# The second feed-forward product in chunks of 2, 3, 2, 2 pairs in place of 2, 2, 2, 3, with fetches for the next chunk begun in a chunk's first unit

## The chip, the core and the metric

The kernel runs on one core of a Trainium2 chip. The metric is the device time of one launch in microseconds (us), as the median of several runs. The engines are named as in the profile: PE multiplies matrices, ACT and DVE work on elements, POOL starts the accumulating transfers, and SP starts nearly all other transfers.

## What is computed

The reference is a decoder trunk of two layers over a stream of 1024 tokens by 1024 features in float32. Each layer has a mixer (in layer 0 a gated convolution beside a matrix memory, in layer 1 a gated unit) and then the feed-forward part, which is all that the change touches:

```python
def swiglu(xn, w_in, w_out):          # xn 1024 x 1024, D_FF = 2816
    h = xn @ w_in
    g, up = h[..., :D_FF], h[..., D_FF:]
    return (jax.nn.silu(g) * up) @ w_out

for layer in range(2):
    x = x + mixer(rmsnorm(x, norm_mix[layer]), ...)
    x = x + swiglu(rmsnorm(x, norm_ffn[layer]), ffn_w_in[layer], ffn_w_out[layer])
return rmsnorm(x, norm_final)
```

## The kernel before

Every float32 product is made of three passes over operands that are cut into a high part (rounded to the fast float32 format) and a low part (the rest): high by high, high by low, low by high. They are the lines 121, 122 and 123, so a "matmul" below is one of these passes, of 128 x 128 weights on 512 columns.

The 2816 hidden features are 22 blocks of 128. The first product makes them block by block. Blocks 0 to 17 form nine pairs, and for these the second product is done by a scheme of seven block products in place of eight: `STEPS` names them, and each takes one of seven sums of weight blocks and one of seven sums of hidden blocks (b11, b21, t2, t1, t3, b22, t4; below, block 0 to 6). The seven sums of hidden blocks of a pair are stored, high and low, in DRAM (`hd`), 14 tiles of 256 KB per pair. Blocks 18 to 21 (the tail, `TAIL = 4`) go through DRAM too (`td`, 16 tiles in all), and are multiplied in the ordinary way at the end (`part`, tiles f0y, weights by line 109).

The second product runs over chunks of pairs, and `PAIRS` says how many pairs each chunk has. In a chunk there are four units (`onto(dp, ch)`, dp = 0 to 3), each of which makes two of the eight row blocks of the output. A unit runs the seven steps; a step has three matmuls for each pair, so that a unit has 42 matmuls in a chunk of two pairs and 63 in a chunk of three. Three PSUM banks a unit (A, B, C) take the products; the function `sink` copies (line 497), subtracts (line 500) or adds (line 490) them. The first chunk leaves its results in the 16 tiles f0x. In every later chunk two of a unit's four results are built in fresh tiles f0e, and POOL adds each to its f0x tile by an accumulating transfer (line 394, `gather`).

For each unit two raw weight tiles st0 and st1 are fetched by SP (line 323). ACT and DVE cut and sum them one unit ahead of their use (lines 329, 330 and 340 to 343). The raw tiles have four buffers, so that the tiles of one unit can be fetched only when DVE is through with those of the unit two before it.

The hidden blocks of a chunk are fetched by SP as well: `bring(ch, i)` fetches block i of chunk ch, two tiles for each of its pairs (line 479, tiles f0h), into a pool of 68 tiles called slots. That pool also holds the 16 f0x tiles and the f0e tiles. A chunk of two pairs needs 28 slots and one of three pairs 42. The tables `spread` and `ending` say after which step of which unit each block of the next chunk (with `ending`, of the tail) is called for. Each entry stands for a unit, and has steps and the blocks called for after them. A scheduler then fixes the order of the instructions on each engine at build time; each engine runs its own in that order and waits on semaphores, and SP too starts its transfers strictly in order.

Names: f0h is followed by pair, block and part (0 high, 1 low), as in f0h630 for pair 6, block 3, high; st0_f0o31 is the first raw weight tile of chunk 3, unit 1; f0e31 is the result tile of row block 3, right half. Layer 1 has the same with f1.

Of the kernel before, what the change touches and what calls it, by code (L numbers as in the profile page):

```python
# [23 lines left out]
NC = S // P  # L24
SLOT = 516
EPS = 1e-6
PAIRS = (2, 2, 2, 3)
TAIL = 4
DIRECT = 2
GELU_C = math.sqrt(2.0 / math.pi)  # L30
# [13 lines left out]
def trunk(ctx, tc, x_t, vecs, b_gate, b_s, ws_t, we, we_v, we_g, we_o, wo_u, wo_v, wo_o, wf_in, wf_out, out_t):  # L44
# [351 lines left out]
    def swiglu(layer, normed, todo, spans, after):  # L396
# [80 lines left out]
        def fetch(at, i, nm):  # L477
            t = slot(nm, F32R)
            nc.sync.dma_start(t[:, :HALF].bitcast(F32), at[i * P : (i + 1) * P, :])
            return t  # L480
# [3 lines left out]
        def onto(dp, ch):  # L484
# [14 lines left out]
            def less(d, c, p, q):  # L499
                nc.vector.tensor_tensor(hold[d, c], p, q, op=ALU.subtract)  # L500
                if not opening:
                    gather(x[d][c][:, :HALF], hold[d, c])

            def sink(s, ps):
# [9 lines left out]
                else:  # L514
                    less(d0, 1, ps, hold[d0, 1])
                if s == 6 and ch == len(PAIRS) - 1:
                    for d in rows:
# [7 lines left out]

        firsts = [sum(PAIRS[:ch]) for ch in range(len(PAIRS))]
        hbs = [{} for _ in PAIRS]
        hl = [[None, None] for _ in range(TAIL)]

        def bring(ch, i):  # L530

            if ch < len(PAIRS):
                hbs[ch][BLOCKS[i]] = [
                    tuple(fetch(hd[p], 2 * i + j, f"{name}h{p}{i}{j}") for j in range(2))
                    for p in range(firsts[ch], firsts[ch] + PAIRS[ch])
                ]
# [13 lines left out]
            w = Halves(wf_in[layer, f], wf_in[layer, NF + f], HALF, f"{name}i{f}")  # L550
            units.append((w, xb, into(f), none if f < NF - 1 else early(0, {s: (s,) for s in range(7)})))
        base = 0
        spread = ({}, {2: (0,), 5: (1,)}, {2: (2,)}, {0: (3,), 2: (4,), 4: (5,), 5: (6,)})
        ending = ({}, {}, {2: (0,)}, {1: (1,)})
        for ch, n in enumerate(PAIRS):
            for dp in range(4):
# [528 lines left out]
    n1, n2, n3 = Scaled("ffn0"), Norm("mix1", True, spill), Scaled("ffn1")  # L1085
    x, todo = even(n1)
    x, todo = swiglu(0, n1, todo, halves, n2)
    x, todo = odd(n2, todo, n3)
    x, todo = swiglu(1, n3, todo, thirds, Final())
    for step in todo:  # L1090
        step()
# [60 lines left out]
```

## Time and profile before

| | us |
|---|---|
| median of three runs | 2099.26 (2099.06 to 2102.05) |
| the profiled execution | 2099.18 |
| its span in the trace | 2097.5 |
| PE busy in the span | 2075.4 (99%) |
| DVE, ACT, POOL busy | 1376.9 (66%), 825.0 (39%), 277.2 (13%) |

The profile is one execution. Its span is from the first to the last instruction seen, and its own time lies 1.68 us above the span. A busy share is time in which the engine had an instruction running; a PE that is busy can still be slow, which the granted clock shows (a mean of 0.996 over the span).

### The profile page before, as it was taken

To read this page: it belongs to the slowest core of one execution; us is meant where nothing else is said; L and a number is where in the kernel's file an instruction comes from. 1 tells how busy PE (TensorE), PEld (TensorE's weight loads), DVE (VectorE), ACT (ScalarE), POOL (GpSimd) and SP (SyncE) were. 2 spreads that over 40 slices of the span, in tenths; PEclk is the share of its full clock that TensorE was granted. 3 is DMA by queue.
4 is the path that set the end of the run, shared out by engine and by line. 5 is a ranking of instruction groups with operands and counts; after the bars stand their busy time and mean duration, and the time that the engine had idled before them with its cause. 6 is when DMAs were issued, how large, how long until landed. Compare 5 with 4: busy or idle time off the path is not lost.

```text
span 2097.5 us, 25504 instructions
## 1 busy us (share of the span) xinstructions
PE 2075.4 (99%) x9294; PEld 1680.6 (80%) x9294; DVE 1376.9 (66%) x2176; ACT 825.0 (39%) x1277; POOL 277.2 (13%) x453
## 2 busy tenths in 40 slices
PE   9999999999999999999999999999999999999998
PEld 7878888888888878877778888888888888877777
DVE  6236566568877777666556666666877777656566
ACT  5111112345444444343235743445444444433234
POOL 0000000003222121101231000002212112001120
PEclk9999999999999999999999999999999999999999
DMA  5121111545444344479994221445534434379993
GB/s 172 61 76 61 46 51 51 189 142 122 179 152 160 131 158 157 156 279 277 309 253 158 91 71 41 169 158 116 184 128 161 160 126 169 114 273 306 322 231 97
DMA packets 131935, 327.89 MB, mean 156 GB/s; under 512 B 17073, under 2 KB 19153, under 8 KB 131809
## 3 DMA queue, kind: packets, MB, share of 16 engines
q1 hardware_dynamic: 88912, 209.77, 29.2%
q0 software_dynamic: 42752, 116.46, 19.2%
q8 instruction: 73, 1.20, 0.2%
q14 instruction: 54, 0.43, 0.1%
q10 hardware_dynamic: 144, 0.03, 0.0%
HBM read 213.98 MB, written 91.24 MB: 146 GB/s over the span
## 4 chain that ended last, share of the span: by engine, by line
PE 89%; issue 5%; DMA 4%; DVE 1%; POOL 1%; ACT 0%; SPq 0%; DVEq 0%; POOLq 0%; ACTq 0%
PE Af1i L121 4%; PE Af1i L122 4%; PE Af1i L123 4%; PE Af0i L121 2%; PE Af0i L122 2%; PE Af0i L123 2%; PE Bf1i L121 2%; PE Bf1i L123 2%; PE Bf1i L122 2%; PE Af1o L121 2%; PE Af1o L123 1%; PE Af1o L122 1%; PE ov L121 1%; PE op L121 1%; PE ou L121 1%
## 5 line engine op out<-in xcount | busy, mean ns | idle before, releaser
L260 POOL DMA_DIRECT2D x_dram<-xe x16 | 8.6, 540 | 450.8 <-DVE xe L274 445.7
L260 POOL DMA_DIRECT2D x_dram<-xo x16 | 8.6, 540 | 276.8 <-DVE xo L274 271.7
L110 ACT CAST hi_eo<-st_eo 128x1024 fp32r<-128x1024 f32 x20 | 21.0, 1049 | 48.9 <-PE ep L122 30.6
L459 DVE TENSOR_TENSOR f0q<-f0q,Af0i 128x512 f32<-128x512 f32 x20 | 13.8, 688 | 35.9 <-PE Af0i L123 35.9
L459 DVE TENSOR_TENSOR f1q<-f1q,Af1i 128x512 f32<-128x512 f32 x20 | 13.7, 687 | 35.7 <-PE Af1i L123 35.7
L394 POOL DMA_DIRECT2D f0x<-f0e x24 | 20.7, 874 | 120.3 <-DVE f0e L500 103.7
L394 POOL DMA_DIRECT2D f1x<-f1e x24 | 21.0, 878 | 117.9 <-DVE f1e L500 95.3
L329 ACT CAST hix_f0i<-st_f0i 128x1024 fp32r<-128x1024 f32 x20 | 21.1, 1053 | 39.2 <-PE Af0i L122 25.1
L329 ACT CAST hix_f1i<-st_f1i 128x1024 fp32r<-128x1024 f32 x20 | 21.0, 1052 | 38.5 <-PE Af1i L122 25.1
L329 ACT CAST hiy_f1i<-st_f1i 128x1024 fp32r<-128x1024 f32 x20 | 21.1, 1053 | 31.3 <-PE Bf1i L122 30.7
L329 ACT CAST hiy_f0i<-st_f0i 128x1024 fp32r<-128x1024 f32 x20 | 21.1, 1055 | 31.1 <-PE Bf0i L122 30.6
L449 DVE TENSOR_TENSOR f1b<-Cf1i,f1b 128x512 f32<-128x512 f32 x20 | 13.8, 689 | 26.6 <-issue 17.9
L449 DVE TENSOR_TENSOR f0b<-Cf0i,f0b 128x512 f32<-128x512 f32 x20 | 13.8, 688 | 26.6 <-issue 17.9
L121 PE MATMUL f1y<-f1h,hi_f1o 128*128 128x256 f32 (+1 forms) x96 | 30.8, 321 | 0.0
L122 PE MATMUL f1y<-f1h,hi_f1o 128*128 128x256 f32 (+1 forms) x96 | 30.8, 321 | 0.0
L110 ACT CAST hi_oo<-st_oo 128x1024 fp32r<-128x1024 f32 x16 | 16.8, 1052 | 35.1 <-PE op L122 26.9
L123 PE MATMUL f1y<-f1h,lo_f1o 128*128 128x256 f32 (+1 forms) x96 | 30.6, 319 | 0.0
L110 ACT CAST hi_evw<-st_evw 128x1024 fp32r<-128x1024 f32 x8 | 8.4, 1050 | 55.5 <-PE ek L122 36.6
L329 ACT CAST hia_f1i<-st_f1i 128x1024 fp32r<-128x1024 f32 x20 | 21.0, 1050 | 22.2 <-PE Cf1i L122 18.4
L329 ACT CAST hia_f0i<-st_f0i 128x1024 fp32r<-128x1024 f32 x20 | 21.0, 1049 | 22.2 <-PE Cf0i L122 18.4
L111 DVE TENSOR_TENSOR lo_eo<-st_eo,hi_eo 128x1024 fp32r<-128x1024 f32 x20 | 24.5, 1223 | 7.5 <-ACT hi_eo L110 7.5
L274 DVE TENSOR_TENSOR xe<-ep,xe 128x512 f32<-128x512 f32 x16 | 11.0, 690 | 27.5 <-PE ep L123 27.4
(3189 smaller groups left out, 7405.5 us busy)
## 6 DMA issues: line engine op xcount, KB each, us to landing
f0h<-hd SPq DMA_DIRECT2D x126, 256.0 KB, 5.8
f1h<-hd SPq DMA_DIRECT2D x126, 256.0 KB, 5.8
st_f0i<-wf_in SPq DMA_DIRECT2D x40, 512.0 KB, 3.5
st_f1i<-wf_in SPq DMA_DIRECT2D x40, 512.0 KB, 3.4
st_eo<-we_o SPq DMA_DIRECT2D x16, 512.0 KB, 3.7
st_oo<-wo_o SPq DMA_DIRECT2D x16, 512.0 KB, 3.5
st_f0o<-wf_out SPq DMA_DIRECT2D x24, 256.0 KB, 3.5
f0x<-f0e POOLq DMA_DIRECT2D x24, 256.0 KB, 6.6
```

Source lines behind the costliest of these rows:

```text
L110: nc.scalar.copy(hi[:, part], st[:, part])
L111: nc.vector.tensor_tensor(lo[:, part], st[:, part], hi[:, part].bitcast(F32), op=ALU.subtract)
L121: nc.tensor.matmul(ps, lhsT=lh, rhs=rh, start=first, stop=False, skip_group_check=more)
L122: nc.tensor.matmul(ps, lhsT=lh, rhs=rl, start=False, stop=False, skip_group_check=more)
L123: nc.tensor.matmul(ps, lhsT=ll, rhs=rh, start=False, stop=last, skip_group_check=more)
L260: nc.gpsimd.dma_start(x_at[0][d * P : (d + 1) * P, c * HALF : (c + 1) * HALF], x[d][c][:, :HALF])
L274: nc.vector.tensor_tensor(x, ps, x, op=ALU.add)
L329: nc.scalar.copy(hi, src)
L394: nc.gpsimd.dma_start(dst, src, accum_op=ALU.add)
L449: nc.vector.tensor_tensor(r, ps, r, op=ALU.add)
L459: nc.vector.tensor_tensor(st["q"], st["q"], ps, op=ALU.subtract)
```

## The change

The chunk of three pairs moves from the last place to the second, and the table of the fetches is a new one. The weights of the second product are laid out by the host from `PAIRS`, so they follow.

```diff
-PAIRS = (2, 2, 2, 3)
+PAIRS = (2, 3, 2, 2)
...
-        spread = ({}, {2: (0,), 5: (1,)}, {2: (2,)}, {0: (3,), 2: (4,), 4: (5,), 5: (6,)})
+        spread = ({5: (0,)}, {2: (1,), 5: (2,)}, {2: (3,)}, {2: (4,), 4: (5,), 5: (6,)})
         ending = ({}, {}, {2: (0,)}, {1: (1,)})
```

Before, block 0 of the next chunk was called for in the second unit, and blocks 3 to 6 in the last. Now block 0 is called for in the first unit, block 3 in the third, and blocks 4 to 6 in the last. The table for the tail stays. Both layers are built alike.

What this makes of the order on SP, at the fetches for the chunk of three pairs: before, that is chunk 3, whose blocks 3 to 6 (24 tiles) stand between the weights of its first and of its second unit.

```order
L323 DMA st0_f0o30_81_7989<-wf_out 128x768
L323 DMA st1_f0o30_81_7990<-wf_out 128x768
L479 DMA f0h630_8003<-hd06_3431 128x512
L479 DMA f0h631_8005<-hd06_3431 128x512
...
L479 DMA f0h860_8103<-hd08_3433 128x512
L479 DMA f0h861_8105<-hd08_3433 128x512
L323 DMA st0_f0o31_82_8118<-wf_out 128x768
L323 DMA st1_f0o31_82_8119<-wf_out 128x768
```

After, it is chunk 1; the same place in the program reads:

```order
L323 DMA st0_f0o10_73_7241<-wf_out 128x768
L323 DMA st1_f0o10_73_7242<-wf_out 128x768
L479 DMA f0h230_7182<-hd02_3427 128x512
...
L479 DMA f0h431_7192<-hd04_3429 128x512
L323 DMA st0_f0o11_74_7358<-wf_out 128x768
L323 DMA st1_f0o11_74_7359<-wf_out 128x768
L479 DMA f0h240_7275<-hd02_3427 128x512
L479 DMA f0h241_7277<-hd02_3427 128x512
...
L479 DMA f0h461_7344<-hd04_3429 128x512
L323 DMA st0_f0o12_75_7468<-wf_out 128x768
```

Six fetches (block 3) stand behind the weights of the first unit, then come the weights of the second unit, and 18 fetches (blocks 4 to 6) follow them.

On ACT, at the second unit of chunk 1, before (a chunk of two pairs); DMAHW names a transfer started by SP, DMASW one started by POOL, and the others the engines:

```order
L497 COPY f0e21_7442<-Af0o11_74_7415 128x512 [waits PE_49]
L329 CAST hix_f0o12_75_7473<-st0_f0o12_75_7411 128x512 [waits DVE_49,PE_49,Activation_49]
L497 COPY f0e31_7458<-Bf0o11_74_7416 128x512 [waits DMAHW6_49]
L329 CAST hiy_f0o12_75_7485<-st1_f0o12_75_7412 128x512 [waits DMAHW5_49,PE_49]
L329 CAST hiz_f0o12_75_7504<-s3_f0o12_75_7468 128x256 [waits PE_49]
```

And after (a chunk of three pairs):

```order
L497 COPY f0e21_7508<-Af0o11_74_7472 128x512 [waits PE_49]
L497 COPY f0e31_7527<-Bf0o11_74_7473 128x512 [waits DMASW1_49,DVE_49,PE_49]
L329 CAST hix_f0o12_75_7545<-st0_f0o12_75_7468 128x768 [waits DVE_49,PE_49,Activation_49]
L329 CAST hiy_f0o12_75_7560<-st1_f0o12_75_7469 128x768 [waits DMAHW7_49,PE_49]
L329 CAST hiz_f0o12_75_7582<-s3_f0o12_75_7540 128x384 [waits PE_49]
```

The copy that makes f0e31 stood behind the first cut of the next unit's weights and waited for an SP transfer; now it stands ahead of that cut and waits for a POOL transfer, which is the accumulating transfer of f0e01, made by the unit before, whose slot it takes.

## Rows read from the trace of the kernel before

**Rows 1.** Page, busy time of each engine: us, share of span, instructions.
```profile
PE 2075.4 (99%) x9294; PEld 1680.6 (80%) x9294; DVE 1376.9 (66%) x2176; ACT 825.0 (39%) x1277; POOL 277.2 (13%) x453
```

**Rows 2.** Windows, layer 0: stretch, busy us, granted PE clock, DMA share, GB/s.
```profile
917.00:927.00 10.00, 10.00 (x43) 7.67 (x43) 5.91 (x11) 4.40 (x9) 0.00 (x0) 1.00 0.69 227
...
1007.00:1017.00 10.00, 10.00 (x45) 8.09 (x44) 7.19 (x12) 3.15 (x5) 1.72 (x2) 1.00 1.07 346
...
1027.00:1037.00 10.00, 7.31 (x26) 4.42 (x25) 1.07 (x2) 0.90 (x2) 1.09 (x2) 0.95 1.07 329
1037.00:1047.00 10.00, 10.00 (x32) 7.68 (x32) 9.93 (x17) 3.41 (x5) 4.12 (x5) 0.71 0.84 149
```

**Rows 3.** Timeline of PE, layer 0: start, duration, instruction, idle time before it.
```profile
877.92 0.39 PE L121 MATMUL Af0i<-x_ffn000h,hia_f0i 128*128 128x512 f32 x1
...
897.34 0.39 PE L121 MATMUL Af0o<-f0h,hia_f0o 128*128 128x512 f32 x1
...
1030.43 0.40 PE L121 MATMUL Af0o<-f0h,hiy_f0o 128*128 128x512 f32 x1
...
1036.64 0.80 PE L121 MATMUL Af0o<-f0h,hia_f0o 128*128 128x512 f32 x1 [1.99 <-ACT hia_f0o L329]
...
1043.13 0.40 PE L121 MATMUL Cf0o<-f0h,hia_f0o 128*128 128x512 f32 x1
...
1051.92 0.39 PE L123 MATMUL Bf0o<-f0h,lox_f0o 128*128 128x512 f32 x1
1052.64 0.50 PE L121 MATMUL Af0o<-f0h,hiy_f0o 128*128 128x512 f32 x1 [0.34 <-DVE f0e L500]
```

**Rows 4.** Timeline of PE, layer 1, the same place.
```profile
1985.09 0.47 PE L121 MATMUL Af1o<-f1h,hiy_f1o 128*128 128x512 f32 x1
...
1991.92 0.79 PE L121 MATMUL Af1o<-f1h,hia_f1o 128*128 128x512 f32 x1 [2.34 <-ACT hia_f1o L329]
...
1995.44 0.39 PE L123 MATMUL Af1o<-f1h,loa_f1o 128*128 128x512 f32 x1
```

**Rows 5.** Chain of waits, 1000 to 1060 us: start, duration, what.
```profile
1020.12 5.56 DMA f0h<-hd
1025.74 9.99 DMA st_f0o<-wf_out
1035.75 0.84 ACT hia_f0o L329
...
1042.18 0.87 DVE lox_f0o L330
```

**Rows 6.** Timeline of SP's queue, layer 0: transfers started, grouped.
```profile
931.41 8.90 SPq L479 DMA_DIRECT2D f0h<-hd  x16
...
989.82 12.79 SPq L479 DMA_DIRECT2D f0h<-hd  x18
...
1004.34 20.72 SPq L479 DMA_DIRECT2D f0h<-hd  x24
1025.74 18.54 SPq L323 DMA_DIRECT2D st_f0o<-wf_out  x6
1053.48 1.97 SPq L109 DMA_DIRECT2D st_f0o<-wf_out  x2
1055.50 21.30 SPq L479 DMA_DIRECT2D f0h<-td  x16
```

**Rows 7.** Line 479 (fetches of hidden blocks), 900 to 1090 us: issue to landing.
```profile
DMA to landing us min/median/max: 2.9/5.9/11.7
```

**Rows 8.** Timeline of PE in layer 0, chunk 1.
```profile
954.44 0.40 PE L121 MATMUL Af0o<-f0h,hiz_f0o 128*128 128x512 f32 x1
```

**Rows 9.** Timeline of POOL: the second accumulating transfer of chunk 1.
```profile
949.36 0.86 POOL L394 DMA_DIRECT2D f0x<-f0e  x1 [0.46 <-DVE f0e L500]
```

**Rows 10.** Tile f0e, 940 to 1000 us: its 11 accumulating transfers, issue to landing.
```profile
DMA to landing us min/median/max: 4.0/5.3/7.8
```

**Rows 11.** Tile f0e, 900 to 1090 us: all 24 of layer 0.
```profile
DMA to landing us min/median/max: 3.6/6.6/13.3
```

## Prediction

> **What bounds the kernel now.** I began with the busy times of the page. PE runs in 2075.4 of 2097.5 us [rows 1], so an edit that moves no work off PE can only win time in which PE waits, or in which it runs at the lower clock. The second step was to find such time in the stretch that the change touches, the second product. On PE's timeline the pitch of undisturbed matmuls comes from the last unit of the first product: 84 matmuls lie between 877.92 and 897.34, which is 0.2312 us each [rows 3]. Against this pitch there is one large loss in layer 0. From 1030.43 to 1043.13 PE starts 24 matmuls in 12.70 us [rows 3]; at the pitch they take 24 x 0.2312 = 5.55, so **7.15 us** are lost. Part of it is idle time, 1.99 us of it in one piece before the first matmul of a new unit, which waits for ACT's cut of the weights. Part is the clock: from 1036.64 on, 15 matmuls take 6.49 us, 0.433 each, where the pitch gives 3.47; the windows show a granted clock of 0.71 over 1037 to 1047 [rows 2], which mixes the lower level (1.2 GHz) and the full one (2.4 GHz). So this idle spell, 7.31 busy out of 10 us [rows 2], cost about 3.0 us more after its end. A small loss follows at 1051.92, 0.72 us to the next matmul, **0.49** too much [rows 3]. Layer 1 has the same loss at its same place: 17 matmuls from 1985.09 to 1995.44 take 10.35 us for 3.93 at the pitch, **6.42** lost [rows 4]. Together 7.15 + 0.49 + 6.42 = **14.06 us**.
>
> The Trainium skill (TensorE: Matmul & The Clock Gate, "Wait — 56ns, not 53.3ns?") has 215.7 ns and 426.7 ns between the starts of two matmuls of 512 columns, at the full and at the lower clock. Here the lower one agrees (0.433), the full one is 0.2312; by the page the 42 matmuls would lose 42 x 0.0155 = 0.65 us more, and I go by the row.
>
> What ends last there is read from the chain of waits: a fetch of 5.56 us from 1020.12, then the weights of the last chunk's second unit, which SP starts at 1025.74 and which land 9.99 us later, then ACT's cut of 0.84 us [rows 5], and PE at 1036.64. The weights are late because SP works in order: before them stand 18 fetches (12.79 us, 0.71 each) and 24 more (20.72 us, 0.86 each) [rows 6], in a stretch in which the DMA engines are full (share 1.07, 346 GB/s) [rows 2]. This is the chunk of three pairs, 42 tiles.
>
> **What the change does, and its sum.** No matmul, copy, subtraction or transfer is added or removed; three steps move.
>
> *The 42 tiles move to the first boundary.* By the order on SP, the weights of the three-pair chunk's second unit now stand ahead of blocks 4 to 6; only 18 fetches follow them. The wait chain above (24 fetches, then the weights) no longer exists in that form. The first boundary also has more room: at 917 to 927 the DMA share is 0.69 [rows 2]. SP comes to the 18 fetches about where 16 fetches begin now, at 931.41 [rows 6], since the buffers ahead of them come free by the same matmuls of chunk 0. They take 18 x 0.556 = 10.0 us (the pace of those 16, 8.90 us), 12.8 (the 18 at 989.82) or 15.5 (the pace of the 24), so the last starts at 941.4 to 946.9. With the median landing of 5.9 us [rows 7] they are there at 947.3 to 952.8. By the new order PE wants block 6 at the 321st matmul, counted from 877.92. The row at 954.44 is the 318th [rows 8], so that is 954.44 + 3 x 0.2312 = 955.1: 2 to 8 us to spare. With the longest landing, 11.7, the worst is 946.9 + 11.7 = 958.6, 3.5 late. I take no loss.
>
> *The later boundaries carry 28 tiles.* With 12 tiles in the burst before a chunk, 12 x 0.71 to 12 x 0.86 = 8.5 to 10.3 us, and weights ahead of them, they resemble the first two boundaries of the kernel before, where PE shows no such stall. So of the 14.06 us I take all as gone; if the weights are late again, up to all of it stays (rivals).
>
> *Chunk 1 holds more slots.* 16 + 42 of 68 are taken, and ten are left for f0e tiles and for early fetches. Hence the new wait that the order on ACT shows: the copy of f0e31 waits for the accumulating transfer of f0e01. That transfer starts now at 949.36 [rows 9], after the 290th matmul; in the new order it is the 320th, so 949.36 + 30 x 0.2312 = 956.3. Landing in this part takes 5.3 us in the median [rows 10], so 961.6, and with at most 0.84 for the copy (the cut of a larger tile [rows 5]) 962.4. PE needs the bank at the 360th matmul, 954.44 + 42 x 0.2312 = 964.2: 1.8 us to spare, and at a landing of 7.8 us 0.7 late. Behind the copy on ACT stand the cuts for unit 2, which PE wants some 30 matmuls (7 us) later. For the same reason "begun in the first unit" comes true in part only: the first fetches of block 2 for chunk 2 wait for accumulating transfers. Other copies of this chunk wait for slots that matmuls of the next unit free just ahead of the need. For these small waits I allow **1 us** over both layers; the bounds are 0 (all in time) and about 4 (each layer 0.7 for this copy and as much for two others).
>
> *The tail gets a shorter lead.* The last chunk is now 4 x 42 = 168 matmuls (38.8 us) in place of 252. Its first tail weights need the buffers that DVE frees after the cut for the third unit, called for near the 743rd matmul; the tail begins at the 822nd, 79 x 0.2312 = 18.3 us later. The cut and sums took 6.5 us for three pairs, from the end of ACT's cut at 1036.6 to the end of lox at 1043.05 [rows 5], so I put 4.3 for two: 14.0 us are left. Two weight transfers (1.97) and four fetches (0.86 each, or 1.33 at the pace of 16 in 21.30) [rows 6] with a landing of 5.9 make 11.3 to 13.2. It fits, barely. I take no loss.
>
> Sum, against the profiled execution: 2099.18 - 14.06 + 1 = **2086.1 us**. Its own time lies 0.08 us under the median of the runs, so the same number holds for the median.
>
> **The rivals.**
>
> *The stall moves to the first boundary.* For it: 18 tiles behind weights are still a burst, and its worst end is 3.5 us late. An idle spell of about 2 us brought 3.0 us of lower clock, so a layer would lose 1 to 6.5 us, and both together 2 to 13: 2087 to 2098, about 2092. Against it: the DMA share there is 0.69, not 1.07.
>
> *The stall stays, at a later boundary or as it was, and the change does not do what it says.* For it: fetches of chunk 2 wait on accumulating transfers, and everything behind them on SP, weights too, waits with them. If half to all of the 14.06 us stays, the time is 2093 to 2100. Against it: these waits should end well before PE's need, since the transfers land in 4.0 to 7.8 us [rows 10].
>
> *The tail is late.* With the longest landing, 1.97 + 3.4 + 11.7 = 17.1 us against 14.0 is 3.1 late, 6 with the clock, in each layer: up to 2098, more likely 2088 to 2094. Against it: most landings are half of that.
>
> *Slower than before.* Place: the copy of f0e31. If the accumulating transfer of f0e01 shares the DMA engines with a burst of fetches, it can take the longest time seen in layer 0, 13.3 us [rows 11]: 956.3 + 13.3 + 0.84 = 970.4, 6.3 us late, 9.3 with the clock, and 18.6 in both layers, 2085.1 + 18.6 = 2103.7. The change ends on the other side when a layer loses over 7.0 us, that is from a landing of about 11.0 us in both. For it: the new table calls for chunk 2's fetches earlier, into this very place. Against it: the 11 transfers before the full stretch landed in at most 7.8. The Trainium skill (DMA: Bandwidth & Descriptors, "Issuing engines are not separate DMA queues") speaks for this rival: transfers started by SP and by POOL run on the same 16 engines and interleave. The trace agrees in kind, with 5.3 us in the quiet part and up to 13.3 over the whole.
>
> **How the numbers follow.** Forecast (all or nearly all of the stall gone, 2083.5 to 2089): 0.66. First boundary: 0.11. Stall stays: 0.10. Tail: 0.06. Slower: 0.07. The predicted time is 2086, and the range 2083.5 to 2097, which holds the forecast and most of the first and third rival and leaves out the last and most of the second. A measurement of this kernel can tell about 0.2%, 4.2 us, from no change. Faster by more than that (under 2095.1) has the forecast, nine tenths of the first and third rival and some of the second: 0.83. Within it lie most of the second rival and the ends of the others: 0.11. Slower (over 2103.5): 0.06.
>
> **What would show it.** Right: in layer 0 no wait of PE over 1 us between 900 and 1070, a granted clock of 1.00 in all windows there, the weights of each chunk's second unit started by SP ahead of a burst, layer 1 alike. The single steps: the 18 fetches begin near 931 and have landed by 953; the transfer of f0e01 starts near 956, and PE's next matmul into that bank near 964 has no idle time before it; the tail's first matmul does not wait for a fetch or for line 110. Wrong: PE idle for over 2 us near 955, 964, 1004 or 1070, with 0.43 us per matmul after it; the first of these would be the fetches of the three-pair chunk, the second the slot of f0e31, the third the held fetches of chunk 2, the last the tail.

## The result: slower, by the tail

| | before | changed |
|---|---|---|
| median, us | 2100.36 (2099.06 to 2102.05, 4 runs) | 2116.64 (2114.93 to 2119.43, 4 runs) |
| ratio, 95% interval | | 1.0079 (1.0064 to 1.0094) |
| profiled execution, its span | 2099.18, 2097.5 | 2117.83, 2116.1 |

The change costs 16.3 us where 13 were to be won. The page of the changed kernel shows that PE's work is the same (PE row, as [rows 1]); what grew is the time in which it waits.

```profile
PE 2078.3 (98%) x9294; PEld 1683.3 (80%) x9294; DVE 1376.5 (65%) x2176; ACT 827.0 (39%) x1277; POOL 277.7 (13%) x453
```

To see where, I take the same instructions of PE in both profiled executions and compare the stretches between them. The next rows are PE's timeline of the changed kernel in layer 0.

```profile
908.14 0.50 PE L121 MATMUL Af0o<-f0h,hix_f0o 128*128 128x512 f32 x1 [1.00 <-ACT f0x L497]
...
922.48 0.50 PE L121 MATMUL Bf0o<-f0h,hiy_f0o 128*128 128x512 f32 x1 [0.52 <-ACT hiy_f0o L329]
...
934.16 0.50 PE L123 MATMUL Bf0o<-f0h,loy_f0o 128*128 128x512 f32 x1 [0.59 <-DVE loy_f0o L330]
...
938.82 0.51 PE L121 MATMUL Af0o<-f0h,hia_f0o 128*128 128x512 f32 x1 [0.69 <-ACT hia_f0o L329]
...
1023.76 0.50 PE L121 MATMUL Af0o<-f0h,hiy_f0o 128*128 128x512 f32 x1 [1.53 <-DVE f0e L500]
...
1085.13 0.40 PE L123 MATMUL Af0o<-f0h,loy_f0o 128*128 128x512 f32 x1
...
1099.46 0.80 PE L121 MATMUL f0y<-f0h,hi_f0o 128*128 128x512 f32 x1 [4.69 <-ACT hi_f0o L110]
...
1122.58 1.86 PE L162 MATMUL ss_mix<-ones,tot_mix 128*128 128x1 f32 x8 [3.97 <-DVE tot_mix L146]
...
1143.63 0.39 PE L121 MATMUL ov<-hi_ov0w,x_mix100h 128*128 128x512 f32 x1
```

And in layer 1:

```profile
1874.67 0.50 PE L121 MATMUL Af1o<-f1h,hix_f1o 128*128 128x512 f32 x1 [1.01 <-ACT f1x L497]
...
2049.27 0.39 PE L123 MATMUL Af1o<-f1h,loy_f1o 128*128 128x512 f32 x1
...
2063.05 0.79 PE L121 MATMUL f1y<-f1h,hi_f1o 128*128 128x512 f32 x1 [4.08 <-ACT hi_f1o L110]
...
2080.83 0.83 PE L162 MATMUL ss_final<-ones,tot_final 128*128 128x1 f32 x6 [2.37 <-DVE tot_final L146]
...
2108.56 1.19 PE L179 MATMUL r_final<-dg_final,ones 128*128 128x128 f32 x4 [1.75 <-DVE dg_final L175]
```

| stretch | before | changed | more |
|---|---|---|---|
| up to PE's first wait in the second product of layer 0 | 905.47 | 908.14 | 2.67 |
| from there to the last matmul of the chunks | to 1083.78, 178.31 | to 1085.13, 176.99 - 1.85 = 175.14 | -3.17 |
| tail of layer 0, to the first matmul of layer 1's mixer | to 1130.41, 46.63 | to 1143.63, 58.50 + 1.85 = 60.35 | 13.72 |
| layer 1 up to the same first wait | to 1860.30, 729.89 | to 1874.67, 731.04 | 1.15 |
| from there to the last matmul of the chunks | to 2037.60, 177.30 | to 2049.27, 174.60 - 1.85 = 172.75 | -4.55 |
| tail of layer 1, to the last norm | to 2090.29, 52.69 | to 2108.56, 59.29 + 1.85 = 61.14 | 8.45 |
| rest | | | 0.38 |

In the changed kernel eight tail matmuls stand ahead of the last matmul of the chunks; the 1.85 us (8 x 0.2312) put them where they belong. Of the 2.67 us at the start 2.5 come from the first waits of the kernel, in its first 35 us, long before the change; in other executions they are shorter or longer. The 1.15 us of layer 1 go with no new wait; they build up over some 2000 matmuls, by less than 1 ns each. So **the chunks won 7.7 us and the tail lost 22.2**.

The tail is read from three views. First the timeline of SP (as [rows 6]):

```profile
934.56 11.33 SPq L479 DMA_DIRECT2D f0h<-hd  x18
...
1062.65 1.57 SPq L109 DMA_DIRECT2D st_f0o<-wf_out  x2
1064.31 18.42 SPq L479 DMA_DIRECT2D f0h<-td  x16
1084.40 2.37 SPq L109 DMA_DIRECT2D st_f0o<-wf_out  x2
1088.42 15.17 SPq L109 DMA_DIRECT2D st_ov0w<-wo_v  x4
```

There are four tail weights. Two go out at 1062.65, then the 16 fetches of the tail, and only then, at 1084.40 and 1086.4, the third and the fourth. These two take long to land (line 109, 1080 to 1088 us):

```profile
DMA to landing us min/median/max: 13.9/14.1/14.4
```

ACT's timeline shows what hangs on them; the casts of line 110 make the high part of a tail weight, those of line 195 are the first step of the next layer's norm.

```profile
1082.55 1.05 ACT L110 CAST hi_f0o<-st_f0o 128x1024 fp32r<-128x1024 f32 x1 [2.55 <-PE Af0o L122]
1098.37 1.04 ACT L110 CAST hi_f0o<-st_f0o 128x1024 fp32r<-128x1024 f32 x1 [14.76 <-DMA st_f0o<-wf_out]
1100.93 1.04 ACT L110 CAST hi_f0o<-st_f0o 128x1024 fp32r<-128x1024 f32 x1 [1.52 <-DMA st_f0o<-wf_out]
1101.88 0.72 ACT L195 ACTIVATE x_mix100h<-f0x,vec 128x512 fp32r<-128x512 f32 x1
1104.53 0.72 ACT L195 ACTIVATE x_mix101h<-f0x,vec 128x512 fp32r<-128x512 f32 x1 [1.41 <-DVE f0x L607]
```

DVE's timeline shows the low part of the third weight (line 111) and the add of the first finished row (line 607), which is behind it:

```profile
1099.44 1.23 DVE L111 TENSOR_TENSOR lo_f0o<-st_f0o,hi_f0o 128x1024 fp32r<-128x1024 f32 x1 [13.18 <-ACT hi_f0o L110]
1100.58 0.69 DVE L607 TENSOR_TENSOR f0x<-f0y,f0x 128x512 f32<-128x512 f32 x1
```

ACT stands for 14.76 us, DVE for 13.18 and PE for 4.69. And the norm stands too: the first row's add is behind the late weight on DVE and starts at 1100.58, and the norm's first step, behind the fourth cast on ACT, at 1101.88. Its eight rows then follow each other at about 2.75 us, and PE, which has caught up with them, waits once more (3.97 us at 1122.58). After each of these two waits PE runs at the lower level of its clock, 1.2 GHz (granted clock 0.52 over 1099 to 1104 and over 1122 to 1128): nine matmuls from 1099.46 to 1103.85 take 4.39 us for 2.08. In layer 0 the tail's losses, as distances of starts less 0.2312, are 4.85 (first wait) + 2.3 (clock) + 4.1 (norm) + 3.6 (the norm's own small matmuls and the clock behind them), less 1.3 that the kernel before loses there as well: 13.6 of the 13.72.

In the kernel before, SP and ACT show the same order with more time. These are two timelines of it, SP's and then ACT's:

```profile
1076.89 0.86 SPq L109 DMA_DIRECT2D st_f0o<-wf_out  x2
```

```profile
1083.44 1.05 ACT L110 CAST hi_f0o<-st_f0o 128x1024 fp32r<-128x1024 f32 x1 [2.58 <-DMA st_f0o<-wf_out]
1087.15 1.05 ACT L110 CAST hi_f0o<-st_f0o 128x1024 fp32r<-128x1024 f32 x1 [2.66 <-DMA st_f0o<-wf_out]
1090.10 0.72 ACT L195 ACTIVATE x_mix100h<-f0x,vec 128x512 fp32r<-128x512 f32 x1 [1.89 <-DVE f0x L607]
```

Here the casts wait 2.6 us each, the norm starts at 1090.10, and no matmul of the tail waits for a weight.

### The profile page after: what moved, and what is told of

Read it like the earlier page. It is cut to its first block, busy times and chain, and to the rows that moved or that the text cites. A ratio compares the mean times of both kernels' runs of the same rounds, so it can differ in the third digit from the quotient of the medians.

```text
span 2116.1 us, 25524 instructions
## 1 busy us (share of the span) xinstructions
PE 2078.3 (98%) x9294; PEld 1683.3 (80%) x9294; DVE 1376.5 (65%) x2176; ACT 827.0 (39%) x1277; POOL 277.7 (13%) x453
## 4 chain that ended last, share of the span: by engine, by line
PE 90%; DMA 5%; issue 2%; DVE 2%; ACT 1%; POOL 0%; SPq 0%; DVEq 0%; ACTq 0%; POOLq 0%
PE Af1i L121 4%; PE Af1i L122 4%; PE Af1i L123 4%; PE Af0i L121 3%; PE Af0i L122 3%; PE Af0i L123 3%; PE Bf1i L121 2%; PE Bf1i L123 2%; PE Bf1i L122 2%; PE Bf0i L122 1%; PE Bf0i L121 1%; PE Af1o L121 1%; PE Bf0i L123 1%; PE Af1o L122 1%; PE Af1o L123 1%
## 5 line engine op out<-in xcount | busy, mean ns | idle before, releaser
L121 PE MATMUL f0y<-f0h,hi_f0o 128*128 128x512 f32 x64 | 27.0, 422 | 4.7 <-ACT hi_f0o L110 4.7
```

The lines of the kernel that those rows point to most:

```text
L121: nc.tensor.matmul(ps, lhsT=lh, rhs=rh, start=first, stop=False, skip_group_check=more)
```

## Experiments

Theory A: the tail loses because the third and fourth tail weights stand behind 16 fetches on SP, and the shorter last chunk leaves too little time for that. Rival B: the last 40 us are full of transfers whatever their order. For the small waits of the changed kernel between 920 and 947 there were theory C (the early call of block 0) and theory D (the larger weights of a three-pair chunk). All ratios are to the kernel before, run on the same chip.

**1. Block 1 of the tail behind the tail weights** (tail_late1).

```diff
-        ending = ({}, {}, {2: (0,)}, {1: (1,)})
+        ending = ({}, {}, {2: (0,)}, {})
...
             ws.append(weights(src, f"{name}o{dp}", n))
+        bring(len(PAIRS), 1)
```

> The changed kernel, but block 1 of the tail (8 fetches) is called for after the four tail weights, so that on SP the third and fourth tail weights stand behind 8 fetches in place of 16. Theory A (the tail waits because SP starts these two weights last, behind all 16 fetches): they start some 8 to 10 us earlier, PE's wait for the cut of the tail weights (4.7 us in layer 0, 4.1 in layer 1) goes or falls under 1 us and with it the lower clock and the later wait for the norm's sums; about 22 us of tail losses in both layers shrink to under 8: 2098 to 2105. Theory B (the DMA engines are full for the last 40 us, and the last chunk of 39 us is too short for its bytes, in whatever order): the same bytes move, the wait only changes its name (a fetch of block 1, an accumulating transfer), 2112 to 2118.

Measured: 2096.42 us (ratio 0.9984, 0.9975 to 0.9993), 20.2 us faster than the changed kernel and a little better than theory A had it. SP's timeline:

```profile
1058.03 1.67 SPq L109 DMA_DIRECT2D st_f0o<-wf_out  x2
1059.79 8.11 SPq L479 DMA_DIRECT2D f0h<-td  x8
1068.94 1.91 SPq L109 DMA_DIRECT2D st_f0o<-wf_out  x2
1070.96 12.91 SPq L479 DMA_DIRECT2D f0h<-td  x8
```

ACT's, at the casts of these weights:

```profile
1080.95 1.05 ACT L110 CAST hi_f0o<-st_f0o 128x1024 fp32r<-128x1024 f32 x1 [3.84 <-DMA st_f0o<-wf_out]
1083.56 1.05 ACT L110 CAST hi_f0o<-st_f0o 128x1024 fp32r<-128x1024 f32 x1 [1.56 <-DMA st_f0o<-wf_out]
1086.50 0.73 ACT L195 ACTIVATE x_mix100h<-f0x,vec 128x512 fp32r<-128x512 f32 x1 [1.89 <-DVE f0x L607]
```

The same bytes move, and the two weights still take 11.9 to 13.0 us to land. But they start 10.9 us after the first two, not 21.75, PE doesn't wait for them, and the norm starts at 1086.50. This is theory A. What is left is one wait for the norm, of 1.18 us in layer 0 and 2.10 in layer 1; in layer 0 DVE waits 0.57 us for the accumulating transfer of the eighth row.

**2. Both blocks of the tail two units earlier** (end_vearly).

```diff
-        ending = ({}, {}, {2: (0,)}, {1: (1,)})
+        ending = ({2: (0,)}, {1: (1,)}, {}, {})
```

> The changed kernel, but the tail's two blocks are called for in the first and second unit of the last chunk in place of the third and fourth, so that on SP all 16 fetches stand ahead of the tail weights, which follow each other. Theory A (order on SP): the third and fourth tail weights start as soon as their buffers come free, near 1072, over 10 us earlier; all or nearly all of the 22 us goes: 2094 to 2099. Theory B (bytes): the fetches leave the full stretch for the one before, which is as full (shares of 0.9 to 1.05), so at most half comes back: 2105 to 2114. If the early fetches delay weights of the last chunk, a new wait of PE for a cut shows up in that chunk.

Measured: 2107.6 us (1.0038, 1.0023 to 1.0053). The tail's waits are gone, but PE's timeline has a new one in the last chunk:

```profile
1072.89 0.80 PE L121 MATMUL Af0o<-f0h,hiz_f0o 128*128 128x512 f32 x1 [5.25 <-ACT f0e L497]
```

The row names a result copy, but ACT has no idle time before that copy. It stands there directly behind a cut of the next unit's weights, and the cut waited for a weight:

```profile
1071.73 0.62 ACT L329 CAST hia_f0o<-st_f0o 128x512 fp32r<-128x512 f32 x1 [7.61 <-DMA st_f0o<-wf_out]
1072.26 0.58 ACT L497 COPY f0e<-Af0o 128x512 f32<-128x512 f32 x1
```

SP had started this weight at 1056.88, behind eight of the early fetches, and it took 14.8 us to land. Layer 1 has the same wait with 5.99 us. Theory A holds for the tail. The time lies in the range of theory B, but by what the last sentence of the expectation names: the early fetches delayed weights of the last chunk, and the wait shows at the copy behind the cut.

**3. Chunks of 2, 3, 2, 2 with the old table** (pairs_only).

```diff
-        spread = ({5: (0,)}, {2: (1,), 5: (2,)}, {2: (3,)}, {2: (4,), 4: (5,), 5: (6,)})
+        spread = ({}, {2: (0,), 5: (1,)}, {2: (2,)}, {0: (3,), 2: (4,), 4: (5,), 5: (6,)})
```

> Chunks of 2, 3, 2, 2 with the old table of fetches. The tail's order on SP is that of the changed kernel, so the tail losses (about 22 us) should stay under both theories of the tail. What it tells apart is the small waits of the changed kernel between 920 and 947 (3.0 us in layer 0, 2.5 in layer 1, for cuts of weights): theory C, that they come from calling block 0 in the first unit (six fetches stand between the two weights of the last unit of chunk 0), says they go, and 2110 to 2114; theory D, that they come from the larger weights of a three-pair chunk, says they stay, 2115 to 2118.

Measured: 2120.34 us (1.0102, 1.0085 to 1.0119), above both expectations. The four small waits stand there with the same lengths (0.52, 0.25, 0.60, 0.69 us), so theory C is out: block 0 isn't called early here. Theory D has the right outcome with a wrong reason: in the changed kernel the first three of these waits are in units of chunk 0, whose cut has 128x512 as before. The order on PE explains these three: this is PE's order before and after around the step on bank B of chunk 0's third unit.

```
before
3897 L122 MATMUL Af0o01_70_7035<-f0h161_6948,hiy_f0o01_70_7015 128x512
3898 L123 MATMUL Af0o01_70_7035<-f0h160_6946,loy_f0o01_70_7016 128x512
3899 L122 MATMUL Cf0o02_71_7134<-f0h111_6808,hia_f0o02_71_7053 128x512
3900 L123 MATMUL Cf0o02_71_7134<-f0h110_6806,loa_f0o02_71_7054 128x512
3901 L121 MATMUL Bf0o02_71_7133<-f0h030_6846,hiy_f0o02_71_7104 128x512
changed
3887 L122 MATMUL Cf0o02_71_7154<-f0h111_6808,hia_f0o02_71_7065 128x512
3888 L123 MATMUL Cf0o02_71_7154<-f0h110_6806,loa_f0o02_71_7066 128x512
3889 L121 MATMUL Bf0o02_71_7153<-f0h030_6846,hiy_f0o02_71_7120 128x512
3890 L122 MATMUL Bf0o02_71_7153<-f0h031_6848,hiy_f0o02_71_7120 128x512
3891 L121 MATMUL Bf0o01_70_7048<-f0h050_6905,hix_f0o01_70_7004 128x512
```

The scheduler has put this step 12 matmuls (2.8 us) earlier, ahead of the last steps of the unit before it, and ACT's cut is not ready. The same step of the next unit, where the second and third wait stand, is 12 matmuls earlier too. The fourth wait, at 938.82, is in the first unit of chunk 1: its step is 6 matmuls earlier, but its cut is also the larger one (0.83 us, where a chunk of two pairs has 0.62), so theory D isn't ruled out there. All six kernels here whose second chunk has three pairs, the changed one among them, have the four waits, and none of the others has them there. No run moves the step back, so this is read from the order and not shown by an experiment; why the scheduler does so wasn't tried.

**4. Chunks of 2, 2, 2, 3 with the new table** (spread_only). The edit is that of the change without its first line.

> Chunks of 2, 2, 2, 3 with the new table of fetches. On SP the weights of the last chunk's second unit now stand ahead of 18 fetches, not behind 24, and the tail stays as in the kernel before. Theory A: the loss of about 7 us a layer at the last boundary goes for the most part and no tail loss comes, so this is faster than the kernel before: 2088 to 2094. Rival: the early call costs waits at the first boundary here too (1 to 3 us a layer), and fetches that wait for accumulating transfers hold the weights behind them: 2096 to 2104.

Measured: 2095.36 us (0.9976, 0.9967 to 0.9986), faster than before, between the two ranges. The stall of [rows 3] is gone, as the weights of the second unit now stand ahead of 18 fetches. But these weights and those of the first unit, the x4 in SP's timeline, stand behind 18 other fetches for that chunk:

```profile
990.35 19.30 SPq L479 DMA_DIRECT2D f0h<-hd  x18
1009.74 2.68 SPq L323 DMA_DIRECT2D st_f0o<-wf_out  x4
```

PE waits for result copies, in layer 0 twice (1.02 us, and this row of PE's timeline), in layer 1 twice as well (3.00 and 0.38):

```profile
1022.79 0.49 PE L121 MATMUL Bf0o<-f0h,hix_f0o 128*128 128x512 f32 x1 [3.12 <-ACT f0e L497]
```

Each of these copies follows on ACT directly on a cut, as in experiment 2. In layer 0 the one cut starts at 1014.56, 0.10 us after a weight landed; the other, at 1021.42, follows DVE's sums of a weight that landed at 1020.19. So weights are late here again. Among the 18 fetches ahead of them SP waited 6.5 us for accumulating transfers out of f0e tiles, which is what the rival says.

**5. Block 0 of the tail one unit earlier, block 1 behind the tail weights** (end_split).

```diff
-        ending = ({}, {}, {2: (0,)}, {1: (1,)})
+        ending = ({}, {2: (0,)}, {}, {})
...
             ws.append(weights(src, f"{name}o{dp}", n))
+        bring(len(PAIRS), 1)
```

> Chunks of 2, 3, 2, 2 and the new table, block 0 of the tail called for in the second unit of the last chunk and block 1 after the four tail weights. On SP the tail weights then have no fetch between them, and 8 fetches ahead. Theory A (order on SP): the rest of the tail loss of the kernel with block 1 late (2.9 us in layer 0, 2.6 in layer 1 over the kernel before) goes: 2090 to 2094. Rival (slots): the 8 fetches taken earlier hold slots that the result copies of the last chunk need, as in the kernel with both blocks early, where PE waited 5.25 us for such a copy: 2096 to 2104.

Measured: 2096.26 us (0.9974, 0.9961 to 0.9986), as experiment 1. The four tail weights now follow each other with no fetch between them, the third at 1068.21, and the norm starts at 1082.91, yet PE still waits for the norm, 2.74 us in layer 0, because DVE stands for 5.34 us ahead of the eighth row's add. Neither side was right: no result copy is late, and the rest of the tail loss isn't the order of the weights. The profile names a matmul as what ended this wait of DVE. But the accumulating transfer on whose semaphore the add waits landed at 1106.96, 0.09 us before the add started at 1107.05; POOL had started it at 1100.83, after two others that took 12.6 and 13.4 us to land. In experiment 1 the same row waits for the same transfer. So this rest is of the kind of rival B: transfers that land late where the engines are full (share 1.03 over 1074 to 1101 us).

**6. Chunks of 2, 2, 3, 2** (p2232).

```diff
-PAIRS = (2, 3, 2, 2)
+PAIRS = (2, 2, 3, 2)
```

> Chunks of 2, 2, 3, 2 with the new table and the tail as in the changed kernel. Theory A: the tail loss comes from a last chunk of two pairs, with two tail weights behind 16 fetches, wherever the three-pair chunk stands: PE waits 4 to 5 us for the cut of tail weights again, and 2110 to 2120. Rival: the tail loss belongs to the place of the three-pair chunk (fetches that are late from there on): PE does not wait at the tail, under 2104.

Measured: 2125.48 us (1.0111, 1.0093 to 1.0129). Two rows of PE's timeline:

```profile
978.18 0.50 PE L121 MATMUL Af0o<-f0h,hiz_f0o 128*128 128x512 f32 x1 [3.16 <-ACT f0e L497]
...
1099.68 0.79 PE L121 MATMUL f0y<-f0h,hi_f0o 128*128 128x512 f32 x1 [5.57 <-ACT hi_f0o L110]
```

The tail's wait is there again, so it belongs to a last chunk of two pairs, not to the place of the three. That the time is above the range goes with the first row: result copies are late twice in each layer, 9.3 us in all. The cause is that of experiment 4: each copy follows directly on a cut, and the weights start at 969.60, behind 18 fetches among which SP waited 6.3 us for accumulating transfers.

**7. Chunks of 3, 2, 2, 2** (p3222_late), with the tail of experiment 1 and the new table.

```diff
-PAIRS = (2, 3, 2, 2)
+PAIRS = (3, 2, 2, 2)
```

> Chunks of 3, 2, 2, 2, new table, block 1 of the tail after the tail weights. The 42 tiles of the three-pair chunk are fetched in the last unit of the first product, 84 matmuls long, and no later boundary has more than 28. Theory: tail as in the kernel with block 1 late (about 3 us a layer), small waits at the first boundary gone or moved, 2092 to 2098. Rival: the first chunk's 42 tiles are late, since the tiles are still being stored there: PE waits for fetches near 897 to 910, over 4 us a layer, 2100 to 2110.

Measured: 2098.56 us (0.9983, 0.9973 to 0.9992), just above the theory's range. No wait for a fetch; PE's first wait in the second product, for a copy into f0x, grew from 1.00 to 2.25 us in each layer. Neither expectation named that.

**8. Chunks as before, blocks 3 to 6 called for one or two steps later** (spread_mid).

```diff
-        spread = ({}, {2: (0,), 5: (1,)}, {2: (2,)}, {0: (3,), 2: (4,), 4: (5,), 5: (6,)})
+        spread = ({}, {2: (0,), 5: (1,)}, {2: (2,)}, {2: (3,), 4: (4,), 5: (5,), 6: (6,)})
```

> Chunks of 2, 2, 2, 3 as before, and the table of before with one edit: block 3 is called for after step 2 of the last unit, block 4 after step 4, 5 after 5, 6 after 6. On SP the weights of the last chunk's second unit now stand ahead of all 24 fetches; nothing is called for earlier. Theory A (the loss of the kernel before is the order of these weights on SP): PE's wait for ACT's cut (2.0 and 2.3 us, with the lower clock after it) goes, and no wait for a result copy comes, as in the kernel with the new table (1.0 and 3.1 us): 2088 to 2093. Rival: the 24 fetches start later and are late in their turn, PE waits for fetches for 2 to 7 us a layer: 2096 to 2108.

Measured: 2094.97 us (0.9967, 0.9955 to 0.998), between the two ranges, nearer theory A, and with experiment 4 the fastest. SP's timeline:

```profile
1004.94 7.34 SPq L323 DMA_DIRECT2D st_f0o<-wf_out  x4
1012.38 21.17 SPq L479 DMA_DIRECT2D f0h<-hd  x24
```

Against [rows 6] the weights of the second unit (the second half of the x4) stand ahead of the 24 fetches in place of behind them. The fetches start 8 us later and still no matmul waits for one. Some waits for result copies are left, 0.7 to 1.9 us, each copy again directly behind a cut, and one of 0.74 us for a cut; in both layers all waits of PE in the chunks make some 6 us.

**9. The kernel before, with the tail of experiment 1** (before_late1).

```diff
-        ending = ({}, {}, {2: (0,)}, {1: (1,)})
+        ending = ({}, {}, {2: (0,)}, {})
...
             ws.append(weights(src, f"{name}o{dp}", n))
+        bring(len(PAIRS), 1)
```

> Control: the kernel before (2, 2, 2, 3, old table), with the one edit of the tail that brought some 20 us in the changed kernel, block 1 of the tail called for after the four tail weights. Theory A: the order on SP costs only where the lead is too short; with a last chunk of three pairs the third and fourth tail weights start near 1077 and land before the tail needs them, so nothing is won: within 2 us of the kernel before. Rival: the edit is worth something wherever it is made (fewer fetches in the full stretch): 2090 to 2096.

Measured: 2101.66 us (1.0002, 0.9993 to 1.0012). The edit that is worth 20 us in the changed kernel is worth nothing with a last chunk of three pairs.

**10. Chunks of 2, 3, 2, 2, old table, tail of experiment 1** (pairs_late1); the edits are those of 1 and 3.

> Chunks of 2, 3, 2, 2 with the old table and block 1 of the tail after the tail weights. With the kernel before, the one with the new table alone (2095.4) and the changed one with block 1 late (2096.4) it makes a square, free of the tail loss. Theory A: as the old table cost 3.7 us against the new one with the tail loss (2120.3 against 2116.6, waits for cuts and result copies near 944 to 958), it costs about as much here: 2098 to 2102. Rival: the difference came from the tail, and there is none here: 2095 to 2097.

Measured: 2102.71 us (1.0012, 1.0002 to 1.0021), a little above the range of theory A. With the tail mended where the chunks are new (by experiment 9 that is worth nothing with the old chunks and the old table), the square is: before 2100.4, new table 2095.4, new chunks 2102.7, both 2096.4. By the ratios the table is worth 5 to 6 us with either order of chunks; the order of chunks wins nothing and costs 1.7 to 2.5 us, hardly clear of the noise, and what is left of the tail loss is in that.

**11. Chunks as before, all blocks later** (spread_late).

```diff
-        spread = ({}, {2: (0,), 5: (1,)}, {2: (2,)}, {0: (3,), 2: (4,), 4: (5,), 5: (6,)})
+        spread = ({}, {5: (0,)}, {2: (1,), 5: (2,)}, {2: (3,), 4: (4,), 5: (5,), 6: (6,)})
```

> Chunks of 2, 2, 2, 3 and every block called for later than before: block 0 after step 5 of the second unit, blocks 1 and 2 in the third, blocks 3 to 6 in the last as in the kernel with the late block 3. On SP the weights of the last chunk's second unit stand behind the 24 fetches again, as in the kernel before. Theory A (the order of these weights): PE waits for their cut again, by 1 to 3 us with the lower clock behind it, and the 14 us of both layers come back for the most part: 2096 to 2102. Rival: in the kernel with the late block 3 it was the lateness of the fetches that helped (free slots), which is greater here: 2090 to 2094.

Measured: 2111.87 us (1.005, 1.0035 to 1.0065), the theory's side, with a loss greater than expected. SP's timeline, then one row each of ACT's, DVE's and PE's:

```profile
998.79 33.16 SPq L479 DMA_DIRECT2D f0h<-hd  x36
1032.32 17.77 SPq L323 DMA_DIRECT2D st_f0o<-wf_out  x6
```

```profile
1037.88 0.83 ACT L329 CAST hia_f0o<-st_f0o 128x768 fp32r<-128x768 f32 x1 [11.38 <-DMA st_f0o<-wf_out]
1038.74 0.96 DVE L330 TENSOR_TENSOR loa_f0o<-st_f0o,hia_f0o 128x768 fp32r<-128x768 f32 x1 [16.29 <-ACT hia_f0o L329]
1040.36 0.80 PE L121 MATMUL Af0o<-f0h,hiy_f0o 128*128 128x512 f32 x1 [6.18 <-DVE f0e L500]
```

Now 36 fetches stand ahead of the weights, which start 6.6 us later than in [rows 6], and PE waits 6.18 us where it waited 1.99. The row names a subtraction on DVE; it stands there behind the low part of the late weight, which follows ACT's cut. Experiment 8, the kernel before and this one are a series: weights ahead of the burst, behind 24 fetches and behind 36 make 2095, 2100 and 2112.

## Why the prediction was wrong

*The stall of 14.06 us.* Right in place and cause: in the changed kernel no matmul of the chunks waits for a fetch, and none for weights behind a burst. Experiments 8 and 11 show the cause by moving only calls of fetches. The price fits too: 14.06 less the some 7 us of small waits below is 7, and the chunks won 7.7.

*The 18 fetches.* Right. They begin at 934.56, which is 931.9 without the 2.67 us of the start; they take 11.33 us, and the longest landing was 5.7 us (line 479, 934 to 946 us):

```profile
DMA to landing us min/median/max: 5.0/5.3/5.7
```

The reason that I gave, a DMA share of 0.69, is not what the windows of the changed kernel show: the earlier calls fill that stretch, without harm.

```profile
917.00:927.00 10.00, 9.48 (x41) 7.20 (x40) 4.75 (x10) 3.91 (x8) 0.00 (x0) 1.00 0.99 367
...
1077.00:1087.00 10.00, 10.00 (x45) 7.89 (x44) 5.54 (x8) 3.17 (x4) 2.23 (x3) 1.00 1.10 261
1087.00:1097.00 10.00, 7.78 (x34) 6.01 (x32) 0.00 (x0) 0.00 (x0) 4.40 (x5) 1.00 1.09 306
```

*The copy of f0e31* (the rival "slower than before"). Right that it costs nothing: the accumulating transfers of this part landed in at most 6.6 us (tile f0e, 940 to 1000 us), and PE has no wait near its place.

```profile
DMA to landing us min/median/max: 3.6/4.6/6.6
```

Nor did a copy without a slot hold PE in experiments 2, 4, 6 and 8: where the profile names a copy there (0.4 to 6.0 us), the copy follows directly on a cut of weights, and where the waits were long these weights were late. What experiments 4 and 6 do show is the mechanism of the rival "The stall stays": fetches wait on accumulating transfers, and the weights behind them on SP wait with them.

*The allowance of 1 us for small waits.* Mis-sized: 4.8 us in layer 0 (0.69, 0.41, 0.76, 0.85 at the first boundary and 1.69 at 1023.76, and less than 0.4 elsewhere, each a distance of starts less 0.2312) and 2.4 in layer 1, about 7 in all. Its cause was not slots. The first three waits come from PE's order, which I had read only at the places of the argument, and the fourth from that or from the larger cut. At 1023.76 the subtraction that PE waits for stands on DVE behind sums of the next weights, for one of which DVE waited 4.80 us.

*The tail, "It fits, barely. I take no loss."* This is the step that failed. The lead was right in kind (the last chunk is shorter by 19 us), but I counted it to the tail's first matmul, two weights and four fetches. All four weights are needed, and in the order that stood before me the third and fourth are behind all 16 fetches. The same rows would have said: 1.97 + 16 x 0.86 to 1.33 = 15.7 to 23.3 us to their start, 9.99 to land [rows 5, 6], so 25.7 to 33.3; PE wants the third at the 889th matmul, 146 x 0.2312 - 4.3 = 29.5 us after the release: from in time to 3.8 us late in each layer, and ACT's cut of 1.05 us comes on top. Measured from the first weight's start, the third started after 21.75 us and landed 13.9 later, and with the cut it was ready after 36.8; PE came to it after 32.1 and waited 4.69. Nor did I ask what stands behind these weights on ACT and DVE: the norm of the next layer, which with the clock made the loss in layer 0 nearly three times the first wait, and in layer 1 twice. So the rival "the tail is late" had the right place, and a price of up to 2098 where 2117 came out. That it is the order, not the bytes, is shown by experiments 1 and 9 together: the same edit of eight fetches gives 20 us here and nothing there.

The Trainium skill (DMA: Bandwidth & Descriptors, "Issuing engines are not separate DMA queues") says that transfers started by SP and POOL run on the same 16 engines and interleave. The trace agrees: the two weights landed in 13.9 to 14.4 us while POOL's accumulating transfers and SP's fetches filled the engines to 1.09 and 1.10. The share alone doesn't set it, though: in the kernel before the same two landed in 6.5 to 9.7 us, at a share of 1.07 (1077 to 1087 us).

## What to carry to other kernels

When a stage gets shorter, look for everything that was fetched under its cover, and count each transfer queue to the last transfer that the next stage needs, with the landing time of the full stretch in which it will run. On each in-order engine, ask what stands behind the instruction that would wait: here a late weight held the next layer's norm as well. When the profile names a copy as what ended a wait, look at what stood ahead of the copy on its engine: in experiments 2, 4, 6 and 8 it was a cut of weights. And a gain from where fetches are called for is best tried by that table alone: calling four blocks one or two steps later (experiment 8) gave as much as any other edit here, with the chunks where they were. The table has its own risk, as experiment 11 shows; what has to be read first is where the weights stand in SP's order.

## What the runs showed of the hardware

The third and fourth tail weight, 512 KB each, landed in 6.5 to 9.7 us in the kernel before, in 11.9 to 13.0 in experiment 1 and in 13.9 to 14.4 in the changed kernel, all at a DMA share of 1.07 to 1.10; the median of the 40 weights of 512 KB of layer 0's first product (st_f0i) in the kernel before is 3.5. So where the engines are full, the share doesn't say how long a transfer takes, and a landing time from the quiet part of a trace can be four times too short. What goes with the landing time is the number of transfers, of SP and POOL together, that have started and not yet landed when the weight starts: 7 and 8 in the kernel before, 10 and 11 in experiment 1, 12 and 11 in the changed kernel. Over the 52 tail weights of layer 0 in the thirteen kernels, 1 to 3 transfers under way go with 4.9 to 6.7 us, and 10 to 12 with 11.2 to 14.7. That the number is the cause wasn't tried.
